# A hybrid encoder on one core: stacks built through a DRAM scratch, softmax's high half on ScalarE, and new costs in the planner that sets the order

## The chip, the cores and the metric

The kernel runs on one core of a Trainium2 chip. The metric is device time in microseconds of one execution of the whole program, taken as the median over runs.

## The reference, cut to what matters

Two request groups of 512 tokens (width 1024) go through two layers with the same weights. Each layer is a norm, one wide input projection, two mixers side by side, gates, and one output projection with a residual:

```python
h = rmsnorm(x, g_norm) * (1.0 + scale) + shift
qa, ka, va, ga, qb, kb, vb, gb = split(h @ w_in)
# mixer A: 8 heads x 64, rotary, three dilated windows merged by their softmax denominators
ya = merge([dilated_attention(rope(qa) / 8, rope(ka), va, w, d)
            for w, d in ((128, 1), (512, 4), (2048, 16))]) * silu(ga)
# mixer B: 4 heads of two-way retention (key dim 64, value dim 128), group norm
yr = headnorm(retention_fwd(qb, kb, vb) + retention_bwd(qb, kb, vb)) * silu(gb)
x = x + gate * (concat([ya, yr]) @ w_out)
```

`scale`, `shift` and `gate` come from a small matrix product of the group's conditioning vector with `w_ada`. A last norm ends it.

## The kernel before, in words

**Precision.** Every large product is done in three matmuls on a high and a low half of each operand (`wH`, `wL`; hi and lo of `hT`), so TensorE streams three 128x512 matmuls for each block of 128 input rows.

**What TensorE does.** Per layer there are 1,536 projection matmuls (`hT` with `wH`, `wL`; 128x512, or 128x256 for the retention values), then 408 matmuls of the output projection (`wo`, `yT`). Between the projection matmuls stands the mixers' work: attention scores (`QS` with `KS`, `KL`), attention's value products (`pT` with `vn`, 24 matmuls a time), retention's scores and products (`sr`, `rv`), and, in the first layer, the `w_ada` products for the modulation (`wa`).

**Weights.** A tile of `w_in` is loaded as `raw` (SyncE's queue), rounded to `wH` on ScalarE, and `wL` is the rest, computed on GpSimd. The same is done with `w_out` (`rawo` to `wo`).

**Stacks.** `rope` rotates the query and key block of a head pair on VectorE, splits it in hi and lo, and then builds six tiles out of 32-partition strips: for each of two heads `QS` (q hi, lo), `KS` (k hi twice) and `KL` (k lo twice), 128x512 each. Each strip is one copy from SBUF to SBUF of 64 KB on SyncE's queue: 24 copies a call, 24 calls in all (4 attention pairs and 2 retention pairs, 2 groups, 2 layers), 576 copies.

**Softmax.** For each block of 128 queries and one head: scores on TensorE; VectorE adds the mask table and takes the row minimum (`sS`, `sm`); ScalarE takes the exponential and its row sum; VectorE inverts the sum (two small instructions for two blocks), writes the high half `pt` (f16) as `sS` times that factor, and the low half as the same product less the high half. There are 128 such blocks (2 layers x 4 pairs x 2 groups x 2 heads x 4 blocks). Four blocks make a pair of `pt` tiles, which a DMA transpose on SyncE's queue turns into `pT` for the value product.

**What sets the order.** The program is recorded in one pass by a planner written in Python (`Plan`). It keeps a clock per engine, adds a cost for each instruction (`Engine.cost`), and at each point puts next whatever task is ready by its clock; main work fills the rest. The order that results is fixed, and every engine runs its own list strictly in order. So costs, in nanoseconds, do not run on the chip; they only decide what stands where. All instructions are issued from one helper, which is why they have one line number in the profile, L377 (L391 in the changed kernel); the names of tiles tell them apart.

Of the kernel before, what the change touches and what calls it, by code (L numbers as in the profile page):

```python
# [10 lines left out]
F32 = mybir.dt.float32  # L11
F32R = mybir.dt.float32r
# [3 lines left out]
AF = mybir.ActivationFunctionType  # L16
ALU = mybir.AluOpType
AX = mybir.AxisListType

P = 128  # L20
# [16 lines left out]
K_STK = 6  # L37
# [87 lines left out]
class Plan:  # L125


    def __init__(self):
        self.free = {"PE": 0.0, "DVE": 0.0, "ACT": 0.0, "POOL": 0.0, "SP": 0.0}
        self.dma = 0.0  # L130
        self.ready = {}
        self.last = {}
        self.slots = {}
        self.dead = set()
        self.tasks = []
# [20 lines left out]
        t = self.at(*tiles)  # L156
        return 0.0 if t <= self.free[eng] else t

    def note(self, eng, cost, outs, ins, nbytes=0.0):
        part = eng == "SP" and outs[0].shape[0] < P  # L160
        outs = [k for a in outs for k in self.keys(a)]
        ins = [k for a in ins for k in self.keys(a)]
        start = self.free[eng]
        for k in ins:
            start = max(start, self.seen(eng, self.ready.get(k)))
        for k in outs:
            if not (part and self.last.get(k, (0.0, ""))[1] == "DMA"):
                start = max(start, self.seen(eng, self.last.get(k)))
        if self.dead.intersection(outs + ins):
            raise RuntimeError("use of a spare buffer")  # L170
        end = start + cost
        self.free[eng] = end
        if eng == "SP":
            self.dma = max(end + 650.0, self.dma) + nbytes
            end = self.dma + 770.0
            eng = "DMA"
        for k in outs:
            self.ready[k] = (max(end, self.ready.get(k, (0.0, ""))[0]), eng)
        for k in outs + ins:
            if end >= self.last.get(k, (0.0, ""))[0]:  # L180
                self.last[k] = (end, eng)
# [185 lines left out]
class Engine:  # L367
# [5 lines left out]
    def __getattr__(self, op):  # L373
        fn = getattr(self.eng, op)

        def call(*args, **kw):
            r = fn(*args, **kw)  # L377
            outs = [a for k, a in kw.items() if k in self.OUT and hasattr(a, "tensor")]
            ins = [a for k, a in kw.items() if k not in self.OUT and hasattr(a, "tensor")]
            pos = [a for a in args if hasattr(a, "tensor")]  # L380
            if "out" in kw:
                ins += pos
            else:
                outs = pos[:1] + outs
                ins = pos[1:] + ins
            nbytes = 0.0
            if self.name == "SP":
                nbytes = outs[0].free_size() * outs[0].shape[0] * (2.0 / 290.0 if outs[0].dtype == F16 else 4.0 / 360.0)
            self.plan.note(self.name, self.cost(op, outs, ins), outs, ins, nbytes)
            return r  # L390
        return call  # L391

    def cost(self, op, outs, ins):
        out = outs[0]
        n = out.free_size()
        psum = any(a.tensor.name.startswith("banks") for a in ins)
        if self.name == "PE":
            c = 0.4219 * n
            self.strip, last = -1, self.strip
            if op == "transpose":  # L400
                return max(108.0, 2 * c)
            if ins[0].dtype == F32:
                if out.shape[0] > 32:
                    return max(4 * c, 60.0)
                self.strip = out.offset // out.ap[0][0] // 32
                return 27.0 if self.strip > last >= 0 else 4 * c
            return 0.5 * c + 14.0 if out.shape[0] == 64 else c
        if self.name == "DVE":
            wide = [a for a in ins if a.free_size() > 1]
            fast = len(wide) <= 1 and not psum and op != "tensor_reduce"  # L410
            if op == "tensor_reduce":
                n = wide[0].free_size()
            return 66.0 + n * (0.53 if fast else 1.05) + (60.0 if fast and len(ins) > 1 and n > 64 else 0.0)
        if self.name == "ACT":
            extra = sum(1 for a in outs[1:]) + sum(1 for a in ins if a.free_size() == 1)
            return (53.0 if psum else 93.0) + 93.0 * extra + 0.833 * n
        if self.name == "POOL":
            return 150.0 + 2.1 * n
        if op == "dma_start_transpose":
            return 1250.0 * n / 1024  # L420
        return 450.0 if any("dram" in str(a.tensor.name) for a in ins + outs) else 650.0
# [3 lines left out]
def trunk_kernel(  # L425
# [8 lines left out]
    plan = Plan()  # L434
# [5 lines left out]
    dp = ctx.enter_context(tc.tile_pool(name="dp", bufs=1, space=bass.MemoryType.DRAM))  # L440
# [5 lines left out]
    H = Heap(plan, cp, "half", NHALF)  # L446
# [392 lines left out]
    def main_wide(pj, job, l, b):  # L839
        for t in range(TT):  # L840
            out = pj[:, t // 2, (t % 2) * 256:(t % 2) * 256 + 256]
            for k in range(KT):
# [5 lines left out]
                T.matmul(out, h, wl, start=False, stop=False)  # L848
                T.matmul(out, lo, wh, start=False, stop=(k == KT - 1))

    def rope(pj, c, s, res, b):
        yield lambda: plan.after("DVE", *pj)
        V.tensor_tensor(c[0], pj[0], cos, op=ALU.mult)
        V.tensor_tensor(s[0], pj[0], sin, op=ALU.mult)
        B_IN.free(pj[0])
        V.tensor_tensor(s[1], pj[1], sin, op=ALU.mult)
        V.tensor_tensor(c[0], c[0], s[1], op=ALU.subtract)
        V.tensor_tensor(c[1], pj[1], cos, op=ALU.mult)
        B_IN.free(pj[1])
        V.tensor_tensor(c[1], c[1], s[0], op=ALU.add)  # L860
        for t in (1, 0):
            yield lambda: plan.after("ACT", c[1 - t])
            A.activation(s[t].bitcast(F32R), c[1 - t], AF.Copy)
        hi, lo = (s[1], s[0]), c
        for t in range(2):
            yield lambda: plan.after("DVE", hi[t])
            V.tensor_tensor(lo[t], lo[t], hi[t], op=ALU.subtract)
        yield lambda: max(plan.at(*hi, *lo) - 1500.0, H.avail(1, 6, K_STK, "R"))
        out = []
        for h in range(2):  # L870
            qs, ks, kl = H.take(1, "QS"), H.take(1, "KS"), H.take(1, "KL")
            for i in range(4):
                Q.dma_start(qs[32 * i:32 * i + 32], (hi, lo)[i // 2][i % 2][32 * h:32 * h + 32])
            for t, src in ((ks, hi), (kl, lo)):
                for i in range(4):
                    Q.dma_start(t[32 * i:32 * i + 32], src[i % 2][64 + 32 * h:96 + 32 * h])
            out.append([x.bitcast(F32R) for x in (qs, ks, kl)])
        res["stk"][b] = out
        H.free(*c, *s)

    def turn(kind, i, b, pj, res):
        rs = res.setdefault((kind[0], i), {"stk": {}, "vv": {}})
# [51 lines left out]
    def soften(p, b, ih, h, sS, tn, res):  # L934
# [8 lines left out]
        ri = tn[:, 4:6]  # L943
        V.reciprocal(ri, tn[:, 2:4])
        V.tensor_scalar(ri, ri, 16384.0, None, op0=ALU.mult)
        for i in range(2):
            V.tensor_scalar(hi[:, i, :], sS[i], ri[:, i:i + 1], None, op0=ALU.mult)
            V.scalar_tensor_tensor(lo[:, i, :], sS[i], ri[:, i:i + 1], hi[:, i, :], op0=ALU.mult, op1=ALU.subtract)
        H.free(*sS)
        pts[0] += 1  # L950
# [437 lines left out]
```

## Time and profile before

| | before |
|---|---|
| median of 3 runs | 1138.96 us (1136.25 to 1142.01) |
| the profiled execution | 1141.08 us, its span 1139.3 us |
| TensorE busy (matmuls) | 1062.7 us, 93% of the span |
| VectorE busy | 855.4 us, 75% |
| ScalarE busy | 388.8 us, 34% |
| GpSimd busy | 193.4 us, 17% |
| mean granted TensorE clock | 0.973 |
| DMA queue of SyncE | 163.55 MB, 55.0% of 16 engines' span |

The span is the time from the first to the last instruction. An engine's busy time is an average over stages with different limits, so the table says which engine is fullest but not where time is lost; for that one asks for busy time by stretch, and for what each engine waited for in it.

### The profile page before, as it was taken

Reading aid. Unit: us, or ns where it says so; the run is one execution under the profiler, and the core shown is the slowest. Engines: PE = TensorE matmul, PEld = TensorE weight load, DVE = VectorE, ACT = ScalarE, POOL = GpSimd, SP = SyncE. Lnnn points to the kernel's source line nnn. Section 1 sums busy time; section 2 is a strip of 40 time slices with the busy share of each in tenths; the row PEclk is TensorE's granted clock in tenths of the full one; section 3 lists DMA queues with packets and bytes.
Section 4 is the critical chain, followed back from the end, with each engine's and each line's share of the span. In section 5 each row is a group of like instructions: output and inputs, shape, how many; then the busy total and the mean of one; then the engine's idle time right before and its main releaser. Section 6 shows DMA issues by size and latency. Waiting matters only on the chain.

```text
span 1139.3 us, 15515 instructions
## 1 busy us (share of the span) xinstructions
PE 1062.7 (93%) x5443; PEld 838.8 (74%) x5443; DVE 855.4 (75%) x1664; ACT 388.8 (34%) x677; POOL 193.4 (17%) x84
## 2 busy tenths in 40 slices
PE   5979999999888989999999999999999999976997
PEld 3757787687766557777888878877887887854886
DVE  5577876688747979889447799589956986797555
ACT  6353314233124313454324333424234233334101
POOL 3052002010120201136000101102111012051000
PEclk9989999999989989999999999999999999987999
DMA  9804877316775756778322386336752477664232
GB/s 316 289 24 139 167 177 230 136 48 163 158 173 143 240 123 149 161 178 259 111 74 75 79 181 162 79 93 149 146 128 65 132 149 167 140 212 102 75 111 74
DMA packets 210429, 164.53 MB, mean 144 GB/s; under 512 B 162032, under 2 KB 172560, under 8 KB 210352
## 3 DMA queue, kind: packets, MB, share of 16 engines
q1 hardware_dynamic: 210352, 163.55, 55.0%
q8 instruction: 43, 0.70, 0.3%
q14 instruction: 34, 0.28, 0.1%
HBM read 79.59 MB, written 8.40 MB: 77 GB/s over the span
## 4 chain that ended last, share of the span: by engine, by line
PE 55%; DVE 25%; SPq 10%; DMA 4%; issue 3%; ACT 2%; POOL 0%; DVEq 0%; ACTq 0%; POOLq 0%
PE banks L377 55%; DVE pt L377 10%; SPq L377 10%; DVE sS L377 2%; DVE rc L377 2%; DVE yr L377 2%; DVE sm L377 1%; DVE th L377 1%; DMA wa<-in_w_ada_dram 1%; DVE hT L377 1%; DVE rsq L377 1%; DMA raw<-in_w_in_dram 1%; DVE sd L377 1%; DVE rs L377 1%; DVE b L377 1%
## 5 line engine op out<-in xcount | busy, mean ns | idle before, releaser
L377 PE MATMUL banks<-hT,wH 128*128 128x512 f32 x1536 | 487.3, 398 | 12.1 <-POOL hT L377 4.4
L377 PEld LDWEIGHTS banks<-hT,wH 128*128 128x128 f32 x1536 | 289.6, 191 | 92.0 <-issue 14.5
L377 PE MATMUL banks<-hT,wL 128*128 128x512 f32 x768 | 303.2, 395 | 3.7 <-POOL wL L377 3.7
L377 POOL TENSOR_TENSOR wL<-raw,wH 128x1024 fp32r<-128x1024 f32 x56 | 139.8, 2505 | 744.4 <-ACT wH L377 577.2
L377 PE MATMUL banks<-wo,yT 128*128 128x512 f32 (+1 forms) x744 | 170.7, 390 | 10.1 <-DVE yT L377 6.9
L377 PEld LDWEIGHTS banks<-hT,wL 128*128 128x128 f32 x768 | 146.5, 191 | 35.1 <-POOL wL L377 4.1
L377 PEld LDWEIGHTS banks<-wo,yT 128*128 128x128 f32 x744 | 139.0, 192 | 40.0 <-DVE yT L377 7.6
L377 PE MATMUL banks<-wH,hT 128*128 128x256 f32 x512 | 96.7, 285 | 0.5 <-ACT wH L377 0.5
L377 ACT ACTIVATE sS<-sS,sm 128x512 f32<-128x512 f32 x76 | 54.3, 715 | 88.2 <-DVE sm L377 78.4
L377 PEld LDWEIGHTS banks<-wH,hT 128*128 128x128 f32 x512 | 81.9, 193 | 2.0 <-ACT wH L377 0.7
L377 DVE SCALAR_TENSOR_TENSOR pt<-sS,sm,pt 128x512 f16<-128x512 f32 x76 | 75.5, 993 | 4.2 <-PE banks L377 1.1
L377 PE MATMUL banks<-wL,hT 128*128 128x256 f32 x256 | 73.1, 285 | 2.2 <-POOL wL L377 2.2
L377 ACT ACTIVATE wH<-raw 128x1024 fp32r<-128x1024 f32 x56 | 58.6, 1052 | 36.8 <-PE banks L377 19.0
L377 DVE CUSTOM_DVE_ANT_0 sS<-banks,tabs 128x512 f32<-128x512 f32 x76 | 49.1, 686 | 18.3 <-PE banks L377 15.9
L377 PE MATMUL banks<-sr,rv 128*128 128x512 f32 x166 | 49.1, 402 | 6.1 <-DVE sr L377 4.7
L377 DVE TENSOR_SCALAR pt<-sS,sm 128x512 f16<-128x512 f32 x76 | 51.4, 676 | 1.6 <-DMA KS<-rc 0.2
L377 PEld LDWEIGHTS banks<-wL,hT 128*128 128x128 f32 x256 | 49.4, 193 | 3.2 <-POOL wL L377 2.4
L377 DVE TENSOR_TENSOR res<-banks,gb 128x512 f32<-128x512 f32 (+1 forms) x33 | 22.1, 670 | 39.4 <-PE banks L377 39.4
L377 POOL TENSOR_TENSOR wo<-rawo,wo 128x1024 fp32r<-128x1024 f32 x16 | 41.2, 2596 | 57.6 <-PE banks L377 29.6
L377 PE MATMUL banks<-pT,vn 128*64 128x512 f16 x384 | 45.8, 383 | 1.6 <-DMA pT<-pt 1.1
L377 ACT ACTIVATE sq<-xr 128x1024 bf16<-128x1024 f32 (+2 forms) x15 | 14.2, 944 | 87.9 <-issue 43.2
L377 PE MATMUL banks<-wa,siluT 128*32 128x128 f32 (+1 forms) x384 | 33.0, 406 | 10.9 <-DMA wa<-in_w_ada_dram 7.9
(326 smaller groups left out, 1384.5 us busy)
## 6 DMA issues: line engine op xcount, KB each, us to landing
raw<-in_w_in_dram SPq DMA_DIRECT2D x56, 512.0 KB, 4.3
wa<-in_w_ada_dram SPq DMA_DIRECT2D x48, 512.0 KB, 4.9
rawo<-in_w_out_dram SPq DMA_DIRECT2D x16, 512.0 KB, 4.5
QS<-rs SPq DMA_DIRECT2D x88, 64.0 KB, 2.0
KL<-rc SPq DMA_DIRECT2D x88, 64.0 KB, 2.0
KS<-rs SPq DMA_DIRECT2D x66, 64.0 KB, 2.0
x1d<-xr SPq DMA_DIRECT2D x8, 512.0 KB, 2.8
xr<-x1d SPq DMA_DIRECT2D x8, 512.0 KB, 4.1
```

The lines of the kernel that those rows point to most:

```text
L377: r = fn(*args, **kw)
```

## The change

Three edits. First, `rope` no longer copies strips from SBUF to SBUF. It writes its four 128x512 results to a DRAM tile (`stk_dram`, 1 MB a call), each as soon as it is ready, and then reads the six stacks from there, one DMA each; rows in a stack come in another order than before, the same in all three tiles of a head. That is 10 DMAs of 256 KB a call, 240 in all. The read waits for the four writes to have landed. Second, the high half of softmax is an activation (copy with a scale per partition) on ScalarE; the low half stays on VectorE. Third, the planner's costs are changed, and it gets a rule that a VectorE instruction with no operand in PSUM and a GpSimd instruction do not run at the same time (`held`). This moves instructions on every engine.

```diff
+    def held(self, eng, start, cost):
+        other = self.port["POOL" if eng == "DVE" else "DVE"]
+        for s, e in other:
+            if s < start + cost and e > start:
+                start = e
...
+        if port:
+            start = self.held(eng, start, cost)
...
-            return 0.5 * c + 14.0 if out.shape[0] == 64 else c
+            return 0.5 * c if out.shape[0] == 64 else c + 12.0
...
-            return 66.0 + n * (0.53 if fast else 1.05) + (60.0 if fast and len(ins) > 1 and n > 64 else 0.0)
+            extra = 0.0
+            if n > 64 and not psum and (op == "scalar_tensor_tensor" or fast):
+                extra = 65.0 * sum(1 for a in ins if a.free_size() == 1) + (60.0 if fast else 0.0)
+            return 66.0 + n * (0.53 if fast else 1.05) + extra
...
-            return 150.0 + 2.1 * n
+            return 30.0 + 2.37 * n
...
-        yield lambda: max(plan.at(*hi, *lo) - 1500.0, H.avail(1, 6, K_STK, "R"))
+        rd = dp.tile([P, 2, 2, 512], F32, name=f"stk_dram{nstk[0]}")
+        for i, x in enumerate((*hi, *lo)):
+            yield lambda: plan.at(x) - 700.0
+            Q.dma_start(rd[:, i % 2, i // 2, :], x)
+        H.free(*c, *s)
+        yield lambda: max(plan.at(rd) - 500.0, H.avail(1, 6, K_STK, "R"))
         out = []
         for h in range(2):
-            qs, ks, kl = H.take(1, "QS"), H.take(1, "KS"), H.take(1, "KL")
-            for i in range(4):
-                Q.dma_start(qs[32 * i:32 * i + 32], (hi, lo)[i // 2][i % 2][32 * h:32 * h + 32])
-            for t, src in ((ks, hi), (kl, lo)):
-                for i in range(4):
-                    Q.dma_start(t[32 * i:32 * i + 32], src[i % 2][64 + 32 * h:96 + 32 * h])
+            q, k = rd[32 * h:32 * h + 32], rd[64 + 32 * h:96 + 32 * h]
+            srcs = [q.rearrange("p j w n -> (p j w) n")]
+            srcs += [k[:, :, w, :].rearrange("p j n -> (p j) n")[:, None, :].to_broadcast([64, 2, 512]) for w in range(2)]
+            ts = [H.take(1, n) for n in ("QS", "KS", "KL")]
+            for t, x in zip(ts, srcs):
+                Q.dma_start(t, x)
...
         for i in range(2):
-            V.tensor_scalar(hi[:, i, :], sS[i], ri[:, i:i + 1], None, op0=ALU.mult)
+            yield lambda: plan.after("ACT", ri)
+            A.activation(hi[:, i, :], sS[i], AF.Copy, scale=ri[:, i:i + 1])
+        for i in range(2):
+            yield lambda: plan.after("DVE", hi[:, i, :])
             V.scalar_tensor_tensor(lo[:, i, :], sS[i], ri[:, i:i + 1], hi[:, i, :], op0=ALU.mult, op1=ALU.subtract)
```

Below, names are those of the tiles; a buffer that is used again keeps the name of its first use, so a stack may be called `nwr`, and a score tile `th`, `sd`, `yr` or `rsq`. `ISA sS,sm<-banks,tabs` is the instruction that adds the mask and takes the minimum.

On SyncE's queue in the first layer, the end of one call's copies and what follows, before:

```order
L377 DMA KS<-sS 32x512
L377 DMA KS<-rc 32x512
L377 DMA raw<-in_w_in_dram 128x1024 x2
L377 DMA_TRANSPOSE pT<-pt 128x16x128 x2
L377 DMA wa<-in_w_ada_dram 128x1024 x2
L377 DMA_TRANSPOSE pT<-pt 128x16x128 x2
L377 DMA raw<-in_w_in_dram 128x1024
```

The two copies shown are the last of 24 in a row. Now one whole call on the same queue, at about the same place in the program:

```order
L391 DMA stk_dram_2479<-rs 128x512
L391 DMA stk_dram_2479<-sd 128x512
L391 DMA stk_dram_2479<-sS 128x512
L391 DMA raw<-in_w_in_dram 128x1024 x2
L391 DMA stk_dram_2479<-yr 128x512
L391 DMA wa<-in_w_ada_dram 128x1024 x2
L391 DMA raw<-in_w_in_dram 128x1024
L391 DMA QS<-stk_dram_2479 128x512
L391 DMA QS<-stk_dram_2479 128x1x512
L391 DMA KL<-stk_dram_2479 128x1x512
L391 DMA KL<-stk_dram_2479 128x512
L391 DMA KS<-stk_dram_2479 128x1x512 x2
```

Weight loads now stand between a call's four writes and its six reads.

On VectorE near the end of the second layer, the softmax of two blocks, before (the second and third line of each pair are the halves):

```order
L377 RECIPROCAL sm<-sm 128x2
L377 TENSOR_SCALAR sm<-sm 128x2
L377 TENSOR_SCALAR pt<-yr,sm 128x512
L377 SCALAR_TENSOR_TENSOR pt<-yr,sm,pt 128x512
L377 TENSOR_SCALAR pt<-rsq,sm 128x512
L377 SCALAR_TENSOR_TENSOR pt<-rsq,sm,pt 128x512
```

And now, on VectorE, and then on ScalarE in the same stretch:

```order
L391 RECIPROCAL sm<-sm 128x2
L391 TENSOR_SCALAR sm<-sm 128x2
L391 SCALAR_TENSOR_TENSOR pt<-th,sm,pt 128x512
L391 SCALAR_TENSOR_TENSOR pt<-sd,sm,pt 128x512
L391 ISA th,sm<-banks,tabs 128x512
```

```order
L391 ACTIVATE sd,sm<-sd,sm 128x512
L391 ACTIVATE sS,sm<-sS,sm 128x512
L391 ACTIVATE th<-banks 128x512
L391 ACTIVATE pt<-th,sm 128x512
L391 ACTIVATE pt<-sd,sm 128x512 x2
```

The high halves have gone from VectorE's list to ScalarE's, behind exponentials and a gate.

On TensorE at the end of the second layer, before:

```order
L377 LDWEIGHTS vn
L377 MATMUL banks<-pT,vn 64x512
L377 MATMUL banks<-wo,yT 128x512 x36
L377 LDWEIGHTS vn
L377 MATMUL banks<-pT,vn 64x512
...
L377 MATMUL banks<-wo,yT 128x512 x324
L377 MATMUL banks<-wo,yT 128x256 x48
```

And now, from the last of attention's value products on:

```order
L391 LDWEIGHTS vn
L391 MATMUL banks<-pT,vn 64x512
L391 MATMUL banks<-hT,wH 128x512 x2
L391 MATMUL banks<-hT,wL 128x512
...
L391 MATMUL banks<-hT,wL 128x512
L391 MATMUL banks<-wo,yT 128x512 x360
L391 MATMUL banks<-wo,yT 128x256 x48
```

Before, the last two value products (24 matmuls each) stood behind the last projection matmul, the second of them inside the output projection; now 102 projection matmuls stand behind the last one. At the end of the first layer the last value product stood 24 matmuls into the output projection, and now 9 projection matmuls ahead of it.

## Rows read from the trace of the kernel before

**Rows 1.** Busy time by stretch: from:to, length, each engine, clock, DMA share, GB/s.

```profile
82.00:285.00 203.00, 201.17 (x1013) 154.72 (x1012) 148.94 (x274) 63.18 (x118) 29.65 (x12) 0.99 0.57 151
285.00:519.00 234.00, 210.85 (x1031) 159.17 (x1030) 187.91 (x324) 78.76 (x147) 42.41 (x18) 0.94 0.69 167
519.00:1010.00 491.00, 486.45 (x2426) 397.68 (x2425) 379.40 (x706) 175.54 (x301) 82.93 (x34) 1.00 0.52 131
1010.00:1045.00 35.00, 17.60 (x63) 11.97 (x62) 33.48 (x49) 16.10 (x31) 13.20 (x6) 0.66 0.66 153
...
sum 1139.30, PE 1062.69 PEld 838.78 DVE 855.41 ACT 388.76 POOL 193.43; mean PE 177.12 PEld 139.80 DVE 142.57 ACT 64.79 POOL 32.24
```

**Rows 2.** The same view of seven stretches, each with the clock at 0.50.

```profile
402.48:412.72 10.24, 8.08 (x22) 4.77 (x23) 10.07 (x20) 2.37 (x3) 0.00 (x0) 0.50 0.90 218
...
1013.47:1023.71 10.24, 5.47 (x13) 4.32 (x14) 10.13 (x17) 4.69 (x11) 4.61 (x2) 0.50 0.91 218
1030.53:1044.19 13.66, 6.69 (x15) 4.82 (x16) 13.48 (x20) 7.09 (x14) 3.29 (x2) 0.50 0.51 94
sum 51.20, PE 36.00 PEld 26.05 DVE 46.79 ACT 17.66 POOL 14.49; mean PE 5.14 PEld 3.72 DVE 6.68 ACT 2.52 POOL 2.07
```

**Rows 3.** TensorE's longest waits (total, times, longest): 1005 to 1045, then 285 to 519.

```profile
PE banks L377 <- DVE sm L377: 7.3, 1, 7.3
PE banks L377 <- DVE yT L377: 6.9, 1, 6.9
...
PE banks L377 <- POOL wL L377: 5.9, 2, 3.7
PE banks L377 <- DVE sr L377: 4.2, 2, 3.6
```

**Rows 4.** Timeline of the second layer's end: start, duration, engine, instruction, [wait before].

```profile
1009.42 0.62 PE L377 MATMUL banks<-hT,wH 128*128 128x512 f32 x2
...
1010.10 0.62 PE L377 MATMUL banks<-hT,wH 128*128 128x512 f32 x2
...
1025.50 16.60 SPq L377 DMA_TRANSPOSE pT<-pt  x4
...
1039.58 5.61 PE L377 MATMUL banks<-wo,yT 128*128 128x512 f32 x14 [6.88 <-DVE yT L377]
```

**Rows 5.** Timeline of SyncE's queue, ScalarE and GpSimd, 292 to 324.

```profile
292.47 0.57 SPq L377 DMA_DIRECT2D QS<-rs  x1
...
308.10 0.59 SPq L377 DMA_DIRECT2D KS<-rc  x1
308.79 1.03 SPq L377 DMA_DIRECT2D raw<-in_w_in_dram  x2
...
312.87 1.06 ACT L377 ACTIVATE wH<-raw 128x1024 fp32r<-128x1024 f32 x1 [4.91 <-DMA raw<-in_w_in_dram]
...
318.34 5.25 POOL L377 TENSOR_TENSOR wL<-raw,wH 128x1024 fp32r<-128x1024 f32 x2 [28.33 <-DMA pT<-pt]
```

**Rows 6.** Groups of VectorE and ScalarE: operation xcount, busy us, mean ns, idle before.

```profile
L377 DVE SCALAR_TENSOR_TENSOR pt<-sS,sm,pt 128x512 f16<-128x512 f32 x76 | 75.5, 993 | 4.2 <-PE banks L377 1.1
L377 DVE TENSOR_SCALAR pt<-sS,sm 128x512 f16<-128x512 f32 x76 | 51.4, 676 | 1.6 <-DMA KS<-rc 0.2
...
L377 ACT ACTIVATE sS<-sS,sm 128x512 f32<-128x512 f32 x76 | 54.3, 715 | 88.2 <-DVE sm L377 78.4 <-issue 9.7
```

**Rows 7.** Timeline of GpSimd and VectorE, 501 to 507.

```profile
501.87 10.14 POOL L377 TENSOR_TENSOR wo<-rawo,wo 128x1024 fp32r<-128x1024 f32 x4 [27.07 <-PE banks L377]
...
504.34 2.59 DVE L377 TENSOR_SCALAR pt<-yr,sm 128x512 f16<-128x512 f32 x1
```

**Rows 8.** DMA issues (count, KB each, us to landing); last, the queue's ns min/median/max.

```profile
KL<-rc SPq DMA_DIRECT2D x88, 64.0 KB, 2.0
...
x1d<-xr SPq DMA_DIRECT2D x8, 512.0 KB, 2.8
xr<-x1d SPq DMA_DIRECT2D x8, 512.0 KB, 4.1
...
L377 SPq DMA_DIRECT2D xr<-x1d x8: 319/376/423, 1022.0 to 1117.0; - x8
```

More of the change, by code (lines that the diff above doesn't have):

```diff
@@ L130, in __init__ @@
         self.dma = 0.0
+        self.port = {"DVE": [], "POOL": []}
         self.ready = {}
@@ L157, in after, with note @@
         return 0.0 if t <= self.free[eng] else t
-    def note(self, eng, cost, outs, ins, nbytes=0.0):
-        part = eng == "SP" and outs[0].shape[0] < P
+    def held(self, eng, start, cost):
[3 more added lines that the diff above has]
+                start = e
+        own = self.port[eng]
+        own.append((start, start + cost))
+        del own[:-64]
+        return start
+    def note(self, eng, cost, outs, ins, nbytes=0.0, port=False):
+        part = eng == "SP" and (outs[0].shape[0] < P or outs[0].tensor.name.startswith("stk"))
         outs = [k for a in outs for k in self.keys(a)]
@@ L388, in call @@
                 nbytes = outs[0].free_size() * outs[0].shape[0] * (2.0 / 290.0 if outs[0].dtype == F16 else 4.0 / 360.0)
-            self.plan.note(self.name, self.cost(op, outs, ins), outs, ins, nbytes)
+            psum = any(a.tensor.name.startswith("banks") for a in ins)
+            port = self.name == "POOL" or (self.name == "DVE" and not psum)
+            self.plan.note(self.name, self.cost(op, outs, ins), outs, ins, nbytes, port)
             return r
@@ L867, in rope @@
             V.tensor_tensor(lo[t], lo[t], hi[t], op=ALU.subtract)
-        yield lambda: max(plan.at(*hi, *lo) - 1500.0, H.avail(1, 6, K_STK, "R"))
+        nstk[0] += 1
+        rd = dp.tile([P, 2, 2, 512], F32, name=f"stk_dram{nstk[0]}")
[4 more added lines that the diff above has]
+        yield lambda: max(plan.at(rd) - 500.0, H.avail(1, 6, K_STK, "R"))
         out = []
         for h in range(2):
-            qs, ks, kl = H.take(1, "QS"), H.take(1, "KS"), H.take(1, "KL")
-            for i in range(4):
-                Q.dma_start(qs[32 * i:32 * i + 32], (hi, lo)[i // 2][i % 2][32 * h:32 * h + 32])
-            for t, src in ((ks, hi), (kl, lo)):
-                for i in range(4):
-                    Q.dma_start(t[32 * i:32 * i + 32], src[i % 2][64 + 32 * h:96 + 32 * h])
-            out.append([x.bitcast(F32R) for x in (qs, ks, kl)])
+            q, k = rd[32 * h:32 * h + 32], rd[64 + 32 * h:96 + 32 * h]
[4 more added lines that the diff above has]
+                Q.dma_start(t, x)
+            out.append([t.bitcast(F32R) for t in ts])
         res["stk"][b] = out
-        H.free(*c, *s)
     def turn(kind, i, b, pj, res):
```

1 line of the change is left out of this document (added).

## The prediction

> **What bounds the kernel now.** I read the table of busy time by stretch first. TensorE is busy 1062.69 of 1139.30 us, so at most 76.6 us are idle, and the table shows where [rows 1]. From 519 to 1010 (most of the second layer) it idles 491.00 - 486.45 = 4.6 us, from 82 to 285 1.8 us: nothing is to be had there. From 285 to 519 (the rest of the first layer) it idles 234.00 - 210.85 = 23.1 us, and in the 35 us from 1010 to 1045 (end of the second layer) 17.4 us. What is left, some 30 us, lies ahead of 82 and behind 1045, where the change touches almost nothing.
>
> Idle time has a second price. In seven stretches between 285 and 1045, 51.20 us together, the granted clock is 0.50, the lower level of 1.2 GHz [rows 2]; they lie in the same two places as the idle time. TensorE is busy 36.00 us in them, and half of that is lost: 5.47 and 6.69 at the second layer's end, so 6.1 us there, and (36.00 - 12.16)/2 = 11.9 us in the five of the first layer. So **the second layer's end** costs 17.4 + 6.1 = 23.5 us, **the first layer from 285 on** 23.1 + 11.9 = 35.0 us, and 58.5 us is all that this change can reach.
>
> Then who is waited for. At 1010 to 1045 VectorE is busy 33.48 of 35.00 us [rows 1], and the two long waits are for it [rows 3]: 7.3 us for the row minima, 6.9 us for the low half of `yT`, which stands in its list behind the last `pt` halves. SyncE's queue then holds four transposes of `pt` for 16.60 us, and the output projection goes on only at 1039.58 [rows 4]. From 285 to 519 the longest waits are 5.9 us for `wL` and 4.2 us for the retention's `sr`, and the smaller ones are nearly all VectorE's [rows 3].
>
> **The copies.** Each copy of a strip holds SyncE's queue for 0.59 us, and the 24 of a call run from 292.47 to 308.69, 16.2 us [rows 5]. Behind them stand the weight loads: `raw` goes out at 308.79, ScalarE waits 4.91 us for it, GpSimd starts `wL` at 318.34, and this is the 3.7 us in the wait for `wL`. Now a call is 10 DMAs. The nearest row for the queue's time is a transfer between DRAM and 128 partitions, 0.376 us [rows 8], so 3.8 us a call, and (16.2 - 3.8) x 24 = 298 us less of the queue's time over the kernel. The queue is no bound in itself; what counts is a load that no longer stands behind 16 us of copies.
>
> Against that the stack now takes two transfers, one behind the other. From the last result to the last stack: before, 16.2 us and 2.0 us to landing [rows 8], 18.2 us. Now a write (0.4 and 2.8 to landing), six reads (2.3) and 4.1 for the last: 9.6 us by rows of 512 KB, where these are 256 KB. From the other side, if transfer times from DRAM are as long as twice these, 0.4 + 5.6 + 2.3 + 8.2 = 16.5 us, still not later than before. So the stack comes 2 to 9 us earlier; I take no gain from it but the loads', since attention works through head pairs one behind the other and most stacks lie waiting. A first read that waits for the writes also holds the queue for up to 2.8 us with whatever is behind it, loads and transposes; 24 x 2.8 = 67 us of the queue at most, far under the 298. On this the Trainium skill ("DMA: Bandwidth & Descriptors", section on the anatomy of one DMA) speaks against the change: most of a transfer's fixed cost of some 2 us is the receipt from the target memory, heaviest for HBM, so a call would pay it twice, 48 us over 24 calls if nothing covered it. The 2.8 us of a whole 512 KB write, receipt included, says that this is the right size, and the 16.2 us of copies that go says that it is more than covered.
>
> **The high half.** 128 instructions at 0.676 us in the mean [rows 6] go from VectorE: 86.5 of its 855.41 us. The mean is high because some stand still beside GpSimd: 2.59 us at 504.34, while GpSimd works on `wo` for 10.14 us from 501.87 [rows 7]. On ScalarE the nearest row is the exponential with an operand per partition, 0.715 us [rows 6]: 128 x 0.715 = 91.5 us on an engine busy 388.76 us, 480 us then, 42%. That lies beside TensorE's work, so I cost it at nothing; its cover is ScalarE's idle time, in the fullest stretch 35.00 - 16.10 us [rows 1]. If the cover is gone, the price falls on what is behind it in ScalarE's list: `wH`, and by it `wL`, which TensorE waited for already. The chain of one block gets two more handovers (factor to ScalarE, high half back to VectorE); both engines have other blocks in between. A rule of the Trainium skill ("Perfetto Trace Analysis", "Optimizing Scalar/DVE Operations") says that VectorE is the faster engine where it has a fast mode and that moving work to ScalarE may make sense when VectorE is saturated; by its mean of 75% it isn't, and the sum would be nothing; by the stretches it is where it matters, 33.48 of 35.00.
>
> **The order.** At the second layer's end 102 projection matmuls now stand behind the last value product, where before two value products stood behind the last projection. Three such matmuls take 0.68 us (1009.42 to 1010.10, [rows 4]), so this is 34 x 0.68 = 23 us of cover, more than the 14.1 us from the issue of the last transposes at 1025.50 to the going on of the output projection at 1039.58. I expect this end to run nearly without a wait: **-21 us** of the 23.5, bounds -15 (the last gates on VectorE still wait a little) and -23.5. The first layer's end has only 9 projection matmuls, 2 us, behind its last value product, so a short wait may stay there.
>
> In the first layer from 285 on, the 5.9 us for `wL` should go with the copies, and the waits for VectorE shrink: it is busy 187.91 of 234 us there, and of the 86.5 us its share by busy time is 86.5 x 187.91/855.41 = 19 us. I take **-20 us** of the 35.0; bounds -8 (the loads' waits and their part of the clock alone) and -33. New waits come with any new order, and the rows of before can't show them; the nearest measure is what the old order left in its best stretch, 4.6 us in 491: **+4 us**, bounds 0 and +15 (as much as half the first layer's loss, put elsewhere).
>
> **The sum.** -21 - 20 + 4 = -37 us. The profiled execution took 1141.08 us with a span of 1139.3; the median is 1138.96, which is 2.1 less than that execution and equal to its span, so I take the sum off the median: 1138.96 - 37 = **1102 us**. All the good ends give -56.5, 1082; all the bad ones -8, 1131.
>
> **The rivals.** (a) All of the reachable loss goes, 1082 us. For it: the second layer's middle shows that this program can run with 1% idle. Against it: the first layer also carries the `w_ada` loads, at a DMA share of 0.69 [rows 1]. (b) ScalarE holds the chain. An activation that waits for VectorE's factor keeps `wH` and the exponentials behind it; ScalarE waited 78.4 us for row minima already [rows 6]. Then the second layer's end gains 15, the first layer 8, and new waits take 5: 1139 - 18 = 1121 us. (c) The change moves the queue without moving the end: GpSimd's 193.43 us stay, whatever two-operand work VectorE has now stands still in place of the high halves (the low half's mean is 993 ns, [rows 6]), and what TensorE waits for is `sr` and `yT` as before: 1139 us, give or take 5. (d) Slower: stacks land later than the order has them. The order is fixed by computed landings, and scores stand on TensorE where the planner believed the stack to be there. Where the queues are full (the stretches at 402 and 1013 show a DMA share of 0.90 and 0.91, [rows 2]), two transfers in series slip twice. In the first layer 23.1 us of idle time brought 11.9 us of half clock, so each us of wait costs 1.5. With half the 24 stacks 3 us late: 12 x 3 x 1.5 = 54 us, 1102 + 54 = 1156 us. It decides from 37/(24 x 1.5) = 1.0 us of wait a stack.
>
> **How the numbers follow.** The forecast (1091 to 1114) has 50%; (a), 1078 to 1091, 15%; (b), 1114 to 1132, 18%; (c) 8%; (d) 9%. About 0.5%, 6 us, is what a measurement of this kernel can tell from no change: faster 0.83, same 0.08, slower 0.09. The range of 1081 to 1129 leaves out the lowest of (a), the top of (b), (c) and (d), some 20%.
>
> **What would show it.** Right: in the changed kernel's table by stretch TensorE idles under 5 us in the 35 us ahead of the output projection of the second layer, and its clock stays at 1.00 there; the first layer's idle time is halved; VectorE's total falls by some 86 us and ScalarE's rises by some 91; no load of `raw` stands behind more than 6 us of stack DMAs; writes to the scratch land in under 3 us. Wrong: long waits of TensorE for a DMA into `QS`, `KS` or `KL` speak for (d); waits for `pt`, `wH` or `wL` with ScalarE as what they hang on speak for (b); a second layer's end with VectorE again full and TensorE waiting for `yT` speaks for (c).

## The result, and the profile after

The changed kernel takes 1107.4 us in the median of 4 runs (1106.2 to 1109.4), the kernel before 1137.6 us beside it (4 runs). The ratio is 0.973, with a 95% interval of 0.970 to 0.977. The forecast was 1102 us, with a range of 1081 to 1129. The profiled execution of the changed kernel took 1106.17 us, its span is 1104.0 us.

First the page of the changed kernel: busy time of each engine, its share of the span and instructions.

```profile
PE 1052.3 (95%) x5443; PEld 832.7 (75%) x5443; DVE 774.1 (70%) x1536; ACT 467.8 (42%) x808; POOL 194.7 (18%) x84
```

VectorE has lost 81 us and ScalarE gained 79, near the 86 and 91 forecast. The next view tells where the time went: busy time by stretch, the same stretches for both kernels (columns as in [rows 1]). Before:

```profile
80.00:285.00 205.00, 202.42 (x1015) 155.29 (x1014) 149.10 (x275) 63.18 (x118) 31.65 (x13) 0.99 0.57 150
285.00:440.00 155.00, 135.40 (x687) 100.86 (x687) 116.64 (x200) 44.00 (x80) 20.79 (x9) 0.92 0.65 164
440.00:545.00 105.00, 101.45 (x473) 78.52 (x469) 94.15 (x158) 46.08 (x82) 36.72 (x14) 0.98 0.76 192
545.00:925.00 380.00, 375.45 (x1906) 309.98 (x1905) 292.06 (x556) 132.74 (x228) 48.92 (x20) 1.00 0.47 116
925.00:1050.00 125.00, 107.60 (x484) 83.13 (x485) 100.89 (x170) 47.58 (x89) 32.12 (x13) 0.90 0.64 156
```

And after:

```profile
80.00:285.00 205.00, 199.65 (x1014) 148.60 (x1013) 143.05 (x264) 83.10 (x152) 29.46 (x12) 0.98 0.73 206
285.00:440.00 155.00, 152.03 (x807) 121.12 (x805) 115.19 (x208) 66.42 (x117) 25.00 (x10) 1.00 0.71 204
440.00:545.00 105.00, 99.87 (x448) 78.08 (x446) 68.89 (x131) 49.10 (x82) 31.23 (x12) 0.97 0.60 157
545.00:925.00 380.00, 371.76 (x1895) 304.84 (x1894) 285.67 (x531) 165.91 (x289) 52.88 (x21) 1.00 0.57 155
925.00:1050.00 125.00, 122.00 (x562) 96.72 (x561) 77.20 (x143) 52.32 (x92) 31.18 (x12) 0.99 0.53 138
```

I count as lost in a stretch TensorE's idle time (length less the first busy column) and half of what it was busy at the lower clock of 1.2 GHz. From 285 to 440 before lost 155.00 - 135.40 = 19.6 us idle and 10.2 us by the clock, 29.8 us; after, 3.0. From 925 to 1050, with the second layer's end, 17.4 + 6.1 = 23.5 before and 4.7 after. These two gave 46 us. But three other stretches lost more than before: 80 to 285 (4.7, now 8.4), 440 to 545 (5.3, now 8.0) and 545 to 925 (4.6, now 9.9), 12 us together. The longest of TensorE's waits in the changed kernel, over the whole span (total, times, longest):

```profile
PE banks L391 <- DVE nwr L391: 11.8, 4, 3.0
PE banks L391 <- DMA wa<-in_w_ada_dram: 7.9, 5, 5.7
...
PE banks L391 <- DVE yT L391: 2.8, 3, 1.1
...
PE banks L391 <- DMA KL<-stk_dram: 1.5, 2, 1.0
...
PE banks L391 <- DMA QS<-stk_dram: 1.2, 1, 1.2
```

The waits for `wL` and `sr` of [rows 3] are gone, those for the row minima are down to 0.7 us, and the stacks (`QS`, `KL`, `KS`) cost 3.0 us. `wa` has hardly a part in the 12 us: it cost 7.9 us before too, and 7.2 of it lies ahead of 80. What has grown is `nwr`, the input of retention's head norm: four waits of 3 us, one for each pair of heads in each layer, three of them (8.9 us) in these stretches. Before it was:

```profile
PE banks L377 <- DVE nwr L377: 3.4, 2, 2.5
```

The timeline of VectorE and GpSimd shows one of the four, from the beginning of the chain of instructions ahead of it (start, duration, engine, instruction):

```profile
221.96 2.70 POOL L391 TENSOR_TENSOR wL<-raw,wH 128x1024 fp32r<-128x1024 f32 x1 [21.49 <-ACT wH L391]
221.99 0.42 DVE L391 TENSOR_SCALAR yr<-rsq 128x512 int32<-128x512 int32 x1
222.44 2.50 DVE L391 TENSOR_SCALAR yr<-yr 128x512 int32<-128x512 int32 x1
...
227.89 0.69 DVE L391 SCALAR_TENSOR_TENSOR yr<-yr,rsq 128x512 f32<-128x512 f32 x1
228.49 2.39 POOL L391 TENSOR_TENSOR wL<-raw,wH 128x1024 fp32r<-128x1024 f32 x1 [3.83 <-ACT wH L391]
228.61 2.82 DVE L391 SCALAR_TENSOR_TENSOR yr<-yr 128x512 f32<-128x512 f32 x1
...
235.30 0.96 PE L391 MATMUL banks<-nwr,selg 128*128 128x512 f32 x3 [2.99 <-DVE nwr L391]
```

VectorE computes a reciprocal square root in 11 instructions in a row. Two of them start while GpSimd works on a `wL`, and each then ends 0.3 to 0.6 us after that `wL`: 2.50 instead of 0.42 us, 2.82 instead of 0.69. The chain is 4.2 us longer than its instructions take alone, and TensorE, with 57 projection matmuls (12.9 us) to do in the meantime, waits 3 us. The same happens in all four chains: two instructions of about 2.5 and 2.8 us in each. The Trainium skill ("SBUF — State Buffer", section "Who interferes with whom") gives the rule behind it: VectorE and GpSimd share one pair of ports under an exclusive lock, which a VectorE instruction needs when it has two inputs in SBUF or runs in a 2-port mode, and the later one waits until the other's instruction is done. The trace agrees, with the two-input instruction at 228.61 that took 2.82 us beside a `wL` of 2.39. Not every row fits: the instruction at 221.99 took its 0.42 us, though the row of a `wL` starts 0.03 us ahead of it.

### The profile page after: what moved, and what is told of

It is laid out like the page before. It is cut to its first block, busy times and chain, and to the rows that moved or that the text cites. A ratio compares the mean times of both kernels' runs of the same rounds, so it can differ in the third digit from the quotient of the medians.

```text
span 1104.0 us, 14884 instructions
## 1 busy us (share of the span) xinstructions
PE 1052.3 (95%) x5443; PEld 832.7 (75%) x5443; DVE 774.1 (70%) x1536; ACT 467.8 (42%) x808; POOL 194.7 (18%) x84
## 4 chain that ended last, share of the span: by engine, by line
PE 73%; DVE 13%; DMA 3%; SPq 2%; issue 2%; ACT 1%; POOL 1%; DVEq 0%; POOLq 0%; ACTq 0%
PE banks L391 73%; DVE yr L391 2%; DVE rsq L391 2%; SPq L391 2%; DVE th L391 1%; DVE hT L391 1%; DVE sd L391 1%; DMA KL<-stk_dram 1%; DVE pt L391 1%; DVE rc L391 1%; DMA wa<-in_w_ada_dram 1%; DVE xT L391 1%; DMA pT<-pt 1%; DMA raw<-in_w_in_dram 0%; DMA KS<-stk_dram 0%
## 5 line engine op out<-in xcount | busy, mean ns | idle before, releaser
L391 PE MATMUL banks<-wo,yT 128*128 128x512 f32 (+1 forms) x792 | 179.5, 388 | 5.1 <-DVE yT L391 2.8
L391 PEld LDWEIGHTS banks<-wo,yT 128*128 128x128 f32 x792 | 146.5, 190 | 36.6 <-DVE yT L391 4.9
L391 ACT ACTIVATE sq<-xr 128x1024 bf16<-128x1024 f32 (+2 forms) x18 | 17.3, 963 | 114.8 <-DVE xr L391 71.0
L391 DVE SCALAR_TENSOR_TENSOR pt<-sS,sm,pt 128x512 f16<-128x512 f32 x65 | 60.9, 977 | 3.4 <-ACT pt L391 2.8
L391 ACT ACTIVATE sS<-sS,sm 128x512 f32<-128x512 f32 x65 | 46.2, 712 | 28.8 <-DVE sm L391 28.0
L391 DVE CUSTOM_DVE_ANT_0 sS<-banks,tabs 128x512 f32<-128x512 f32 x65 | 42.3, 687 | 19.7 <-PE banks L391 19.6
L391 ACT ACTIVATE pt<-sS,sm 128x512 f16<-128x512 f32 x65 | 43.2, 710 | 5.6 <-DVE sm L391 3.3
```

## The experiments

**Theory:** the copies' time on SyncE's queue and VectorE's time in the softmax held the same two places, so the two edits pay together, and the planner's numbers are worth little. **Rivals:** one edit brings nearly all; or each pays for itself; or what pays is merely another order. Last, the four waits for `nwr` are the new waits of the forecast, and can be taken away.

For the kernels below I give the loss as defined above, so that one can see where it lies (us; the last column is the ratio to the kernel before, with its interval). The stretches are fixed times, so a slower kernel is a few us further back in its program. Ahead of 80 us, outside the table, e2, e4, e8 and e12, which have another latency constant in the planner, lose 15 us, the others 19 to 23.

| kernel | 80:285 | 285:440 | 440:545 | 545:925 | 925:1080 | ratio |
|---|---|---|---|---|---|---|
| before | 4.7 | 29.8 | 5.3 | 4.6 | 23.5 | 1 |
| after | 8.4 | 3.0 | 8.0 | 9.9 | 4.7 | 0.973 (0.970 to 0.977) |
| e1, without the DRAM scratch | 10.4 | 10.8 | 12.8 | 14.5 | 5.1 | 0.994 (0.992 to 0.996) |
| e2, without ScalarE's high half | 15.1 | 1.5 | 35.5 | 12.1 | 5.5 | 0.998 (0.996 to 0.999) |
| e3, with the old costs | 9.5 | 7.2 | 6.5 | 12.8 | 2.6 | 0.977 (0.974 to 0.981) |
| e4, the new costs alone | 11.7 | 22.6 | 24.1 | 21.5 | 1.9 | 1.015 (1.011 to 1.019) |
| e5, the DRAM scratch alone | 12.8 | 5.2 | 42.3 | 10.0 | 6.3 | 1.010 (1.007 to 1.013) |
| e6, ScalarE's high half alone | 7.6 | 38.1 | 13.9 | 10.6 | 1.9 | 1.010 (1.006 to 1.013) |
| e7, the norm's matmul later | 8.7 | 4.7 | 7.4 | 9.2 | 3.5 | 0.972 (0.969 to 0.975) |
| e8, latency constant 220 | 13.8 | 6.4 | 7.6 | 12.0 | 0.2 | 0.974 (0.970 to 0.979) |
| e11, planned clock 4.2 us later | 5.1 | 0.0 | 20.3 | 1.9 | 0.9 | 0.966 (0.964 to 0.967) |
| e12, the same with 3.9 us and 205 | 7.9 | 4.4 | 11.1 | 4.2 | 1.4 | 0.966 (0.964 to 0.967) |

### Each edit undone

**e1**: the changed kernel with the 24 copies a call.

```diff
-            Q.dma_start(rd[:, i % 2, i // 2, :], x)
...
+                Q.dma_start(qs[32 * i:32 * i + 32], (hi, lo)[i // 2][i % 2][32 * h:32 * h + 32])
...
+                    Q.dma_start(t[32 * i:32 * i + 32], src[i % 2][64 + 32 * h:96 + 32 * h])
```

> The changed kernel with the stacks built by the 24 copies from SBUF to SBUF again; ScalarE's high half and the planner's new costs stay. Theory (every edit carries a part; the copies' part is the wait for wL behind them, 5.9 us idle and its half clock): about 1115 us, with SyncE's queue some 250 us fuller. Rival A (the copies were the main thing): 1125 or more. Rival B (the DRAM path buys nothing that matters): 1107 within 4.

Measured: 1130.8 us. Without the scratch 23 of the 30 us are gone.

**e2**: the changed kernel with the high half back on VectorE; with its latency constant of 200 the planner finds no order, so it has 205.

```diff
-            A.activation(hi[:, i, :], sS[i], AF.Copy, scale=ri[:, i:i + 1])
+            V.tensor_scalar(hi[:, i, :], sS[i], ri[:, i:i + 1], None, op0=ALU.mult)
```

> The changed kernel with softmax's high half on VectorE again; DRAM stacks and the planner's new costs stay (the planner's latency is 205 instead of 200, since with 200 it finds no order). Theory: VectorE 86 us fuller, ScalarE 91 us emptier, about 1118 us, most of the difference where VectorE is fullest. Rival A (ScalarE's part is the main thing): 1125 or more. Rival B (the order alone does it, an order made for this load would hide the high half too): 1107 within 4.

Measured: 1134.4 us; 27 of the 30 us are gone. The two edits' shares together are more than the whole: neither is the main one. What each is worth by itself is asked below.

**e3**: both edits, with the planner's old costs and without `held`.

```diff
-            start = self.held(eng, start, cost)
...
-            return 30.0 + 2.37 * n
+            return 150.0 + 2.1 * n
```

> DRAM stacks and ScalarE's high half, with the planner's costs and rules of the kernel before. Theory: some waits come back since the order no longer knows of GpSimd's blocking, about 1114 us. Rival A (the planner's numbers are the main thing): 1125 or more. Rival B (they only shuffle the order): 1107 within 4.

Measured: 1112.7 us, so beside both edits the new numbers are worth 5 us.

**e8**: the changed kernel in a slightly different order.

```diff
-LAT = 200.0
+LAT = 220.0
```

> The changed kernel with one number of the planner moved that means nothing on the chip: the latency it adds to a task's readiness, 220 ns instead of 200. It gives another order of the same work. Theory: within 5 us of 1107. Rival (the gain is the luck of one order): 8 us or more above it.

Measured: 1109.1 us. This one nudge to the order moves the time by some 2 us, far less than the 23 and 27.

### Each edit alone

**e5**: of the change's diff only the hunk in `rope` (and the line by which the planner knows the new DMAs). **e6**: only the hunk with `A.activation`. **e4**: only the hunks in the planner, with the latency constant at 205, since it finds no order with 200.

> Before with the stacks through the DRAM scratch alone; the high half stays on VectorE and the planner's costs are the old ones. Theory (the two edits pay together: SyncE's queue and VectorE each hold the same places, and with one of them left the other's relief is not collected): VectorE busy stays near 855 us, the second layer's end still waits some 7 us for its row minima and some 7 us for yT, and the time is 1131 to 1140 us, at most 0.5% below before. Rival (each edit pays for itself, and only the new planner's order spoils an edit that is alone): 1115 to 1125 us, the first layer from 285 on down by 10 us or more.

> Before with the high half on ScalarE alone; 24 copies a call and the old costs stay. Theory (they pay together): VectorE busy falls to about 775 us, ScalarE rises to about 468 us, and yet loads still stand behind 16 us of copies; the time is 1128 to 1138 us. Rival (each edit pays for itself): 1110 to 1122 us. In either, the second layer's end should lose less than its 23.5 us of before if VectorE alone held it; if it loses as much, it was the queue's transposes and the order that held it.

> Before with the planner's new costs and its rule on the shared port alone (its latency constant at 205 instead of 200, without which it finds no order). The engines' work is as before. Theory (the costs are worth about 5 us whatever else is there): 1129 to 1137 us. Rival (the costs pay only where the two other edits leave room): 1136 to 1145 us.

Measured: 1149.1, 1148.2 and 1154.0 us. Neither theory nor rival had this: each part alone makes the kernel **slower**, by 1.0, 1.0 and 1.5%. The table says how. All three cure the second layer's end (6.3, 1.9 and 1.9 instead of 23.5 us), and all three pay more than that ahead of it: e5 and e6 mostly in the first layer, e4 half in the first layer and half in the second (21.5 instead of 4.6 us from 545 to 925). In e4 only the planner's numbers are new, and that alone makes an order 15 us slower; its longest waits are for `pT`, 33.6 us in all, and what puts them there wasn't followed.

With the copies still there (e6) the loss is from 285 to 440. Its timeline of SyncE's queue, and of TensorE's matmuls on `pT`:

```profile
300.46 0.54 SPq L377 DMA_DIRECT2D QS<-rs  x1
...
316.75 1.87 SPq L377 DMA_TRANSPOSE pT<-pt  x1
318.72 1.02 SPq L377 DMA_DIRECT2D QS<-rs  x1
...
333.72 0.59 SPq L377 DMA_DIRECT2D KS<-modsb  x1
334.41 4.63 SPq L377 DMA_TRANSPOSE pT<-pt  x2
...
338.91 1.06 PE L377 MATMUL banks<-pT,vn 128*64 128x512 f16 x4 [9.33 <-DMA pT<-pt]
```

Two calls' 48 copies hold the queue from 300.46 to 334.31. One transpose gets out between them, and the next, which the same value product needs, stands behind the second call: TensorE waits 9.33 us for it.

With VectorE's high half still there (e5) the middle is nearly as good as after (5.2 us), but the loss comes back from 440 to 545. Its timeline there, of GpSimd, VectorE and SyncE's queue:

```profile
482.46 0.75 DVE L377 SCALAR_TENSOR_TENSOR pt<-sS,sm,pt 128x512 f16<-128x512 f32 x1
482.70 10.37 POOL L377 TENSOR_TENSOR wo<-rawo,wo 128x1024 fp32r<-128x1024 f32 x4 [29.60 <-ACT wo L377]
...
485.60 2.51 DVE L377 TENSOR_SCALAR pt<-sS,sm 128x512 f16<-128x512 f32 x1
...
488.14 2.71 DVE L377 SCALAR_TENSOR_TENSOR pt<-sS,sm,pt 128x512 f16<-128x512 f32 x1
...
493.03 5.27 POOL L377 TENSOR_TENSOR wL<-raw,wH 128x1024 fp32r<-128x1024 f32 x2
493.39 2.71 DVE L377 SCALAR_TENSOR_TENSOR pt<-sS,sm,pt 128x512 f16<-128x512 f32 x1
...
502.13 14.57 SPq L377 DMA_TRANSPOSE pT<-pt  x4
502.77 0.68 DVE L377 SCALAR_TENSOR_TENSOR sS<-sS,banks 128x512 f32<-128x512 f32 x1
```

GpSimd rounds `wo` and `wL` there in one piece, and the softmax of a late head pair runs into it: seven of VectorE's instructions in 18 us last 2.1 to 2.7 us, each about as long as one of GpSimd's. TensorE waits 16.4 us for the bank that VectorE reads at 502.77, and 12.2 us for `pT` behind the transposes. So in these two the loss moves on to what the other edit would have relieved. With the old costs throughout, the ratios are 1.010, 1.010 and, with both edits (e3), 0.977. In the changed kernel the softmax is far enough ahead: its last halves end at 473.7 us, as GpSimd's burst begins (last value product at 484 instead of 540 us in e5).

With the new costs throughout, the same four combinations read otherwise: 1.015 with neither edit (e4), 0.998 with the scratch (e2), 0.994 with the high half (e1), 0.973 with both. There each edit pays for itself, 20 and 23 us, and both together pay 47. So the rival that each pays for itself holds with the new costs and falls with the old, and the costs, worth 5 us beside both edits, are worth 15 to 17 beside one and lose 15 by themselves. That an edit alone loses is thus a matter of the order it gets. How much of the 1 to 1.5% is the luck of one order isn't known: no nudge like e8 was run on the kernel before, e4, e5 or e6.

### The load without a new order

The kernels above differ from each other in order too. The next two keep the changed kernel's order on every engine and add load that the planner doesn't know of.

**e9**:

```diff
+        dd = dp.tile([18, 32, 128], F32, name=f"dose_dram{nstk[0]}")
+        for j in range(18):
+            Q.eng.dma_start(dd[j], small[32 * (j % 4):32 * (j % 4) + 32, :128])
```

> The changed kernel in its own order on every engine, with 18 small DMAs (32 rows of 512 bytes of a constant, to a DRAM tile that nobody reads) put on SyncE's queue behind the six reads of each call, without the planner's knowledge. At the 0.35 to 0.59 us that a DMA holds the queue elsewhere here this is 6 to 11 us a call, 150 to 255 us of the queue in all, and hardly any bytes. Theory (the time that the 24 copies held the queue was itself the cost, by the loads and transposes behind them): TensorE waits for pT, wa, wH or wL come back, and the time rises by 12 to 25 us to 1119 to 1132. Rival (what the copies cost was the order and the stacks' own lateness; the queue has room): 1106 to 1112 us.

Measured: 1217.7 us, ratio 1.070 (1.068 to 1.073): not 12 to 25 but 110 us more than after. SyncE's queue at one of the 24 calls, and the longest of TensorE's waits:

```profile
122.27 8.90 SPq L907 DMA_DIRECT2D dose_dram<-small  x18
131.26 0.85 SPq L391 DMA_DIRECT2D wa<-in_w_ada_dram  x2
132.22 4.02 SPq L391 DMA_TRANSPOSE vn<-vt  x1
```

```profile
PE banks L391 <- DMA pT<-pt: 33.7, 11, 5.3
PE banks L391 <- DMA wa<-in_w_ada_dram: 30.5, 6, 6.8
```

**e10**:

```diff
             yield lambda: plan.after("DVE", hi[:, i, :])
+            V.eng.tensor_scalar(lo[:, i, :], sS[i], ri[:, i:i + 1], None, op0=ALU.mult)
```

> The changed kernel in its own order, with one more VectorE instruction ahead of each of the 128 low halves (the same product as the high half that ScalarE now makes, written to where the low half then goes), without the planner's knowledge: VectorE carries again the 80 to 87 us that the change took from it, ScalarE keeps its part. Theory (VectorE's time in the softmax was the cost): VectorE busy near 855 us, waits for pT and yT at the first layer's end come back, and the time rises by 15 to 27 us to 1122 to 1134. Rival (VectorE has room at 70%; what counted was the order made with the lower load): 1106 to 1114 us.

Measured: 1148.2 us, ratio 1.009 (1.007 to 1.011): 41 us more than after, with VectorE busy 837.4 us, 63 more. `DVE th` (here mostly score tiles) is the longest of TensorE's waits, with 19.1 us (6.7 in the changed kernel).

Both loads cost, so the queue's and VectorE's time do count, and the rivals fall. The one that another order is all that pays falls with e10: nearly VectorE's old load (837.4 of 855.4 us) in the new order is slower than before. But the price was far off. In e9 the 24 rows hold the queue for 225 us (8.5 to 11.1 each) and cost 110 us, 0.5 us for each. In e1, where the planner knew of the copies, the queue has about (16.2 - 6) x 24 = 245 us more (a call's ten DMAs take some 6 us now, below), and they cost 23 us, 0.1 for each. For VectorE it is 41/63 = 0.6 unplanned, and in e2 27/86 = 0.3 planned. With the old costs the same two loads cost some 36 us each (e6 and e5 against e3), 0.15 and 0.4. So time that the order was laid out for cost less here than the same time unannounced, by far for the queue, less clearly for VectorE. That the laying out is the reason is argued: the added loads also stand at other places in the lists than the planned ones.

### The new waits

**e7**:

```diff
-            yield lambda: max(plan.at(hl), B_BG.avail())
+            yield lambda: max(plan.at(hl) + 3200.0, B_BG.avail())
```

> The changed kernel with one edit to the order: the matmul of retention's head norm that follows VectorE's chain for the reciprocal square root is placed 3.2 us later by the planner's clock. In the changed kernel TensorE waits there four times, 11.8 us in all, and beside at least two of these waits the clock is at its lower level for 3.4 us. Theory (these waits are the new ones that the prediction put at 4 us; they go and nothing is late in their place): waits for nwr under 2 us, TensorE idle about 10 us less, 1091 to 1099 us. Rival (the wait only moves, to yT or to the next stacks, as each us given to the norm is taken from what stands behind it): 1104 to 1110 us.

Measured: 1105.7 us. The rival holds. The wait for `nwr` is 0.2 us, but TensorE's waits for `sd` and `rs` are 5.0 and 3.6 us now, at the same place:

```profile
236.27 0.73 PE L391 MATMUL banks<-nwr,selg 128*128 128x512 f32 x2 [1.49 <-DVE rs L391]
...
238.19 0.79 PE L391 MATMUL banks<-nwr,selg 128*128 128x512 f32 x1 [1.19 <-DVE sd L391]
```

The matmul has moved by 6 projection matmuls and 6 scores only, VectorE is still 4 us late, and now what it does behind the chain, freeing banks, is what TensorE waits for.

**e11**: the planner is told that VectorE is late.

```diff
         rsqrt(t[1], t[0], u)
+        plan.free["DVE"] += 4200.0
```

> The changed kernel with one number in the planner: behind the chain for the reciprocal square root VectorE's planned clock is put 4.2 us later, the time by which GpSimd's wL stretched that chain in the trace. The matmul that needs it then stands 75 instead of 57 projection matmuls behind the one ahead of the chain, and all that follows is planned from there. Theory (the waits for nwr, 11.8 us, and the half clock beside them were a misjudged duration, and go once the planner has it): waits for nwr under 1 us, 1091 to 1099 us. Rival (the time saved comes back as other waits, as when the matmul alone was placed later): 1103 to 1109 us.

Measured: 1099.4 us. All four waits for `nwr` are gone, and from 545 to 1080 TensorE loses 2.8 us instead of 14.6. The theory's 1091 to 1099 is just missed, since the first layer's end got worse, 20.3 us instead of 8.0. Its last value product now stands inside the output projection, and TensorE waits 12 us there for ScalarE's `yT`. The timeline of ScalarE and GpSimd:

```profile
477.19 4.83 ACT L391 ACTIVATE wo<-rawo 128x1024 fp32r<-128x1024 f32 x5
...
478.31 15.78 POOL L391 TENSOR_TENSOR wo<-rawo,wo 128x1024 fp32r<-128x1024 f32 x6 [13.59 <-ACT wo L391]
...
485.79 2.94 ACT L391 ACTIVATE wH<-raw 128x1024 fp32r<-128x1024 f32 x3
488.63 1.04 ACT L391 ACTIVATE wo<-rawo 128x1024 fp32r<-128x1024 f32 x1
489.58 1.14 ACT L391 ACTIVATE yT<-th 128x512 fp32r<-128x512 f32 x2
490.25 2.07 PE L391 MATMUL banks<-wo,yT 128*128 128x512 f32 x4 [11.99 <-ACT yT L391]
```

`yT` stands behind a row of `wo` and `wH` on ScalarE.

**e12**: of the orders that small changes of the two numbers give, one with the last value product 27 projection matmuls ahead of the output projection.

```diff
-LAT = 200.0
+LAT = 205.0
...
+        plan.free["DVE"] += 3900.0
```

> The changed kernel with VectorE's planned clock put 3.9 us later behind the chain for the reciprocal square root (before: 4.2), and the planner's latency constant at 205 instead of 200. Of the orders near the last one this is one in which the last value product of the first layer stands 27 projection matmuls ahead of the output projection (9 in the changed kernel; in the run with 4.2 us it stood inside the output projection, and TensorE then waited 12 us for yT). Theory (the wait at the first layer's end came from that place in the order): that end loses 8 us or less instead of 20, the waits for nwr stay under 1 us, and the time is 1084 to 1094 us. Rival (it comes from the rounding of wo, 16 us of GpSimd and 6 of ScalarE in one piece, wherever the value product stands): 16 us or more are lost there, and the time is 1096 to 1102 us.

Measured: 1098.8 us. Inconclusive: that end loses 11.1 us, between the 8 of the theory and the 16 of the rival. The time is the rival's, because the 9 us gained there, and 4 ahead of 80, are offset by 7 us more from 80 to 440 and 3 from 545 to 1080. e11 and e12 can't be told apart (0.966 both); both beat before and after. How much of the first layer's end could go with `yT` ahead of `wo` on ScalarE wasn't tried.

## Why the prediction was right, and where it was not

- **What can be reached.** Forecast: 58.5 us, of which the sum takes 37. The spans of the two traces differ by 35.3 us. Of the 5.4 us between 1102 and 1107.4, 2.1 are the sum, as the two profiled executions differ by 34.9 us and not 37. The rest is the step that put the sum on the median: the profiled execution of before (1141.08 us) was at the slower end of its runs, 2.1 above the median, and that of the changed kernel was the fastest of its four, 1.2 below.
- **The second layer's end, -21.** It gave 18.8. The cover of projection matmuls was the right place to look. But the reading that VectorE, busy 33.48 of 35.00 us [rows 1], was the limit there fell: e4, with all of VectorE's old load and only 6 projection matmuls behind its last value product, loses 1.9 us. What e4, e5 and e6 share there is that no value product stands behind the last projection any more; so the order of before held this end. (e4 loses 17 us more earlier, from 545 to 925.)
- **The first layer, -20.** It gave 24.1 (285 to 545: 35.1 to 11.0). The size was near, and the two causes right. But the forecast let each contribute by itself, the loads' 5.9 us and VectorE's 19; that holds with the new costs (e4, e2, e1) and not with the old (e5, e6). And of what stood behind the copies it named the weight loads; e6 and e9 show the transposes of `pt` as the greater part. The trace of before had it already: in [rows 5] `wH` is done at 313.93, and the bracket says that `wL`, which starts at 318.34, was released by a transpose. In the chain that ended last, that transpose follows the copies and the load (start, duration, what):

```profile
309.93 8.07 DMA pT<-pt
```

- **New waits, +4.** This term was mis-sized: 9.0 us (80 to 285 and 545 to 925), where the waits for `nwr` went from 0.9 to 8.9 us. The old order's best stretch was no measure of it. The row that was one is in [rows 7]: 2.59 us for an instruction beside GpSimd's. The question to ask of it was which chains of such instructions have TensorE right behind them.
- **The planner's rule.** The forecast took the order as given. `held` should have kept the two engines apart, but in the four chains GpSimd's `wL` runs beside the chain, and e3, without `held`, has the same four waits, 11.8 us. The planner only knows of instructions it has already recorded; that the `wL` was recorded later, and held back in the plan instead, is argued from the code, not shown. e11, where 4.2 us more in the plan take the four waits away, shows that it was off there.
- **ScalarE at no cost.** Right: no wait for `wH` or `wL` is left, and rival (b) fell. The forecast priced the halves by their means, 0.676 us on VectorE and 0.715 on ScalarE. The means hid a difference, as two groups of the changed kernel show (count, busy us, mean ns):

```profile
L391 DVE SCALAR_TENSOR_TENSOR pt<-sS,sm,pt 128x512 f16<-128x512 f32 x65 | 60.9, 977 | 3.4 <-ACT pt L391 2.8 <-PE banks L391 0.5
L391 ACT ACTIVATE pt<-sS,sm 128x512 f16<-128x512 f32 x65 | 43.2, 710 | 5.6 <-DVE sm L391 3.3 <-issue 1.7 <-ACT sS L391 0.5
```

  ScalarE's 0.710 us is the mean of each of its `pt` groups within 2 ns, whatever GpSimd does: 23 of its 128 halves overlap an instruction of GpSimd's, and the slowest of them took 0.72. VectorE's halves, 0.49 and 0.75 us alone, are 2.5 and 2.7 beside it.
- **The copies.** A call holds the queue for some 6 us, not 3.8: its six reads take 4.1 us (301.31 to 305.40 in the timeline below), and a write 0.4 in the mean. Writes land in 2.5 to 5.3 us in the median, by source tile, not in under 3. And the queue's own waits show that it stood still for one of them for up to 5.7 us, more than the bound of 2.8, though for all of them together 58 us, under the 67:

```profile
301.31 0.91 SPq L391 DMA_DIRECT2D QS<-stk_dram  x2
302.32 1.18 SPq L391 DMA_DIRECT2D KL<-stk_dram  x2
303.55 1.85 SPq L391 DMA_DIRECT2D KS<-stk_dram  x2
```

```profile
SPq L391 <- DMA stk_dram<-th: 12.4, 5, 5.7
```

  Little of this reached TensorE: stacks cost it 3.0 us in all, 0.1 us for each of the 24 calls, and rival (d), which decides from 1.0, fell.

## What to carry to other kernels

In a program whose order is laid out by computed durations, ask of every edit not only what load it removes but what the order believes: load it knows of cost 0.1 to 0.4 us a microsecond here, load it did not know of 0.5 to 0.6. When an engine's wait is cured and the time doesn't move, look at the next place in program order before giving the edit up: here, with the old costs, each of two edits alone lost 1%, and both together won 2.3%, 2.7% with the planner's new numbers. Such a verdict on one edit holds only for the order it was tried in: with the new costs each of the two gained by itself. And when a wait stands behind a chain that ran longer than planned, correct the chain's duration in the plan, not the place of the one instruction that waited.

## What the runs showed of the hardware

- VectorE's instructions on 128x512 tiles in SBUF, one- or two-operand, lasted about as long as the GpSimd instruction they met, one by one: 0.42 to 2.50, 0.49 to 2.57, 0.69 to 2.82 us, and even a two-column one, 0.17 to 2.17. A burst of GpSimd's work thus turns a row of VectorE's into one at GpSimd's pace, while ScalarE's keep theirs. So do VectorE's instructions with an operand in PSUM: in the changed kernel 68 of them overlap GpSimd's work, with a median of 0.68 us, and it is 0.69 for the others.
- The time that a DMA held SyncE's queue went by the DMA, not by its bytes: 18 of 16 KB took 8.90 us, 0.49 each with the gaps, and two reads of 256 KB 0.91. The Trainium skill ("DMA: Bandwidth & Descriptors", section "Issuing engines are not separate DMA queues") says that the time to initiate a DMA is usually small beside the DMA itself. Here it decided the time: 0.5 us each, in rows of 18, made 110 us.
